# Fixing the order of the last rows on VectorE, with output gates read from PSUM and an early small exponential, in a one-core hybrid decoder layer

## The chip, the cores and the metric

The kernel runs on one core of a Trainium2 chip. The metric is the device time of one execution in microseconds (us), lower is better. In the profile the core's engines are PE (TensorE, matrix products), PEld (its weight loads), DVE (VectorE), ACT (ScalarE), POOL (GpSimd) and SP (SyncE, which issues most DMAs). Each engine runs its own instructions strictly in its own order and waits for others by semaphores.

## The reference

One layer of a decoder, for a prompt of 512 rows and for 8 samples of 4 rows each (32 sample rows), with a model width of 1024, all in float32. Cut to what matters:

```python
h = rms_norm(x, g_mix_pre); z = h @ w_in                   # mLSTM q, k, v, o, gates; attention q, k, v
h_ml = rms_norm(mlstm(q, k, v, gates), g_ml_head) * sigmoid(o)      # o: the output gates, 4 heads x 128
h_da = rms_norm(diff_attend(rope(dq), rope(dk), dv), g_da_head) * (1 - lam_init)
x = x + rms_norm(concat(h_ml, h_da) @ w_out, g_mix_post)
q = rms_norm(x, g_mem_pre) @ w_mq                           # 4 heads x 256
p = softmax(q @ mk.T / 16)                                  # 256 memory tokens; samples: a cached mk and mv each
x = x + rms_norm((p @ mv) @ w_mo, g_mem_post)
u = rms_norm(x, g_ffn_pre) @ w_up                           # 2 x 2752 columns
c = causal_depthwise_conv3(u); a, g = split(c)
x = x + rms_norm((silu(g) * a) @ w_down, g_ffn_post)        # the last line is the tail
# rms_norm(x, g) = x * (mean(x*x) + 1e-6) ** -0.5 * g
```

For the prompt, mk and mv are computed from 256 memory tokens that are normed first (the memory norm). The outputs are the new rows, and the keys, values and states of the layer.

## The kernel before

The 512 prompt rows are four row groups of 128 (b = 0 to 3), and the 32 sample rows are group 4. Weights are streamed from memory. A DMA on SP brings a 512 KB piece into a staging tile `wst`; ACT casts it to a reduced type (line L146), and DVE takes the rest (`split`, L147) into a weight tile `wslot`. Every product is computed as three matmuls, high times high and the two mixed ones. The class `Weights` (`W`) holds four such slots and issues the next load when one is freed; `W.last` is the last weight DMA issued.

Instructions of each engine are put in order by a scheduler from the order of the code, buffers and its own estimates. `tc.issue_after(x)` says that what stands inside may not be put ahead of instruction x; `tc.high_priority()` and `burst` move pieces forward. Generators (`yield`) interleave stages. Tiles come from pools that turn around a few buffers: `N` (5 wide row tiles), `T2`, `Z`, `sm` (small columns), `S` (11 large ones), and PSUM tiles `mm` and `at`.

The places in question are these.

- *Root of the mean square.* `rstd` returns a small tile `rs` with the sum raised to the power -0.5 on POOL (L304). The memory norm at the start copies it on DVE into `mrs` (L540, twice); the norm behind cross-attention copies it into `rsd` (L1178, five times).
- *Output gates.* The projection gives `soT`, four heads x 544 columns, from PSUM by an ACT copy per head and part (`ev_T`, L659). Later `out_gate` takes the sigmoid of each head on ACT (L1031), followed by a product on POOL. The prompt's differential attention then runs: keys are transposed on PE into `tpk` and copied out as `kT` (L1230, ACT and DVE in turn), and exponentials are taken by ACT (`da_soft`, L1261). Sigmoid and exponential need different function tables on ACT, so an ACT_TABLE_LOAD stands between them.
- *Cross-attention.* `ch_soft(i)`, i = 0 to 7 (head and pair of row groups): scores on PE (`sca`), the maximum on DVE (`cnm`), exponentials on ACT, the reciprocal (`csu`) and the shares `cp` on DVE (L1465); `ch_turn` then transposes `cp` on PE (`cpt`, L1474), and `ch_out` multiplies by the values (`cpo`). In between lies the same attention of the samples. The cached keys of sample b arrive as two tiles of 128 x 1024 (`wst` for b < 3, `kvt` from 3 on), are turned in 32 x 32 blocks on DVE (`mk_turn`, L1508), and PE takes the scores `ssc` from them (L1528). `ql` is the low part of the queries (L1439).
- *The tail.* The last group of weight pieces of `w_down` closes the row sums `yp` (prompt) and `ys` (samples). `chunk(b, n0)` is 12 matmuls for one row group and half of the columns, 512 wide; the last half, of group 3, is done as two pieces of 256. `add_y` adds the PSUM tile to `yp` or `ys` on DVE (L1884), ACT takes the square with its row sum `yss` (L1896), and `zy`, the product with the gain g_ffn_post, is taken by POOL for the first half and by DVE for the second (L1898). The sample rows lie on four partition ranges; ACT copies two of each half into `yf` (L1888), DVE copies the others into `yft` (L1890) and adds them (L1891). `end(b)` adds the two sums with epsilon on DVE (L1958, for the last group L1946 and L1947), takes the root on POOL, and adds `zy * rs` to the rows `xf`: by ACT and POOL (L1964, L1965) for the first halves of groups 0 and 1, otherwise by one DVE instruction (L1967, L1955). Each half is written out by a DMA on SP. The rows come back before that (`x_back`, L1975): two groups early, three more after the last weights, in the order 4, 0, 1, 2, 3.

PE's order in the tail is (0, 0), (4, 0), (4, 512), (0, 512), then both halves of groups 1, 2 and 3. The code states DVE's work per row group; the scheduler sets its order.

Of the kernel before, what the change touches and what calls it, by code (L numbers as in the profile page):

```python
# [77 lines left out]
def kernel(ctx: ExitStack, tc: tile.TileContext, I, O):  # L78
# [219 lines left out]
    def rstd(ss, n, w, dim, name="rs"):  # L298

        r = small(w, name)  # L300
# [3 lines left out]
        GTT(out=r[:n], in0=ss, in1=mhalf[:n, :w], op=ALU.pow)  # L304
# [724 lines left out]
    def out_gate():  # L1029
        for h in range(H):  # L1030
            ACT(out=soT[:, h], in_=soT[:, h], func=AF.Sigmoid)  # L1031
# [87 lines left out]
    def proj_add(xt, gname, src, gname2, dst, order=None, scale=None):  # L1119
# [52 lines left out]
        def rows_of(x, n, c0):  # L1172
# [5 lines left out]
            VCP(out=rs[:n], in_=rstd(sumsq(x, n, Z("sqx").bitcast(BF16)[:n]), n, 1, DM))  # L1178
# [266 lines left out]
    pTs, cps, scored = {}, {}, [None]  # L1445

    def ch_soft(i):
# [16 lines left out]
        for j in range(2):  # L1464
            VTS(out=p[:, j, :], in0=p[:, j, :], scalar1=su[:, j:j + 1], scalar2=None, op0=MUL)  # L1465
# [387 lines left out]
    for gi, js in enumerate(groups):  # L1853
# [21 lines left out]
        def add_y(b, ps, n0, w=512):  # L1875
# [9 lines left out]
            if b == 4 and last:  # L1885
                for e in range(2):
                    c = slice(n0 + 256 * e, n0 + 256 * e + 256)
                    nc.scalar.copy(out=yf[:, c], in_=y[NS * e:NS * e + NS])  # L1888
                    t = T2([NS, 256], "yft")
                    VCP(out=t, in_=y[64 + NS * e:64 + NS * e + NS])  # L1890
                    VTT(out=yf[:, c], in0=yf[:, c], in1=t, op=ADD)  # L1891
            if last:
                n = rows(b)[1]
                y = y if b < 4 else yf[:, n0:n0 + 512]
                ss = yss[b, n0] = sm.tile([P, 1], F32, name="yss", tag="yss", bufs=7)[:n]
                ACT(out=Z("sqj")[:n, :w], in_=y, func=AF.Square, scale=DM ** -0.5, accum_out=ss)  # L1896
                z = zs[b, n0] = T2([P, w], "zy")[:n]
                (VTT if n0 else GTT)(out=z, in0=y, in1=gf[:n, n0:n0 + w], op=MUL)  # L1898

        yss, zs = {}, {}  # L1900
        if last:
            yf = N("yf")[:NS]
# [25 lines left out]
        wd = []  # L1928

        def chunk(b, n0):  # L1930
            while len(wd) < (nk // 2 if n0 == 0 else nk):
# [1 line left out]
            w = 256 if (b, n0) == (TORD[-1], 512) else 512
            for o in range(0, 512, w):
                ps = mmp()[:, :w]
                for i in range(0, nk, 2 if b == 4 else 1):
                    t = one(b, ps, i, wd[(n0 and nk // 2) + i // 2], slice(o, o + w))
                add_y(b, ps, n0 + o, w)
            return t

        def end(b):
            c0, n = rows(b)
            xb = xf[b]
            out = O["y_prompt"][0, c0:c0 + n, :] if b < 4 else O["y_sample"].rearrange("b t d -> (b t) d")
            if b == TORD[-1]:
                VTT(out=yss[b, 0], in0=yss[b, 0], in1=yss[b, 512], op=ADD)  # L1946
                STT(out=yss[b, 768], in0=yss[b, 0], scalar=EPS, in1=yss[b, 768], op0=ADD, op1=ADD)  # L1947
# [115 lines left out]
```

## Time and profile before

| | |
|---|---|
| median of 3 runs | 935.84 us (933.85 to 938.36) |
| the profiled execution | 933.45 us |
| its span in the trace | 931.7 us |
| granted TensorE clock, mean | 0.996 |
| PE busy | 913.5 us, 98% |
| DVE busy | 606.5 us, 65% |
| ACT busy | 377.7 us, 41% |
| POOL busy | 223.0 us, 24% |
| moved by DMA | 130.59 MB, mean 140 GB/s |

The span is the time from the first to the last instruction that the trace shows; the profiled execution's own time is 1.75 us longer, and 2.39 us below the median of the runs. Busy times are sums over an engine's instructions. In a row of the timeline stand the start in the span, the busy time of the row, the engine, the line, the operation, what it writes and reads, its shape and how many instructions the row joins, and in brackets how long the engine was idle before it and what released it.

### The profile page before, as it was taken

The numbers are of one execution on the slowest core, as the hardware profiler recorded it, in microseconds if no ns is written. First come the engines' busy times: TensorE is split into PE (matmuls) and PEld (weight loads), VectorE is DVE, ScalarE is ACT, GpSimd is POOL, SyncE is SP. The second block draws the span as 40 slices with busy tenths as digits, with TensorE's granted clock in tenths as the row PEclk, the third lists the DMA queues.
The fourth block names the chain that finished last, engine by engine and source line by source line (L and its number), as shares of the span: only waits on it lengthen the run. The fifth ranks groups of instructions, "written<-read, shape, count | busy, mean of one in ns | idle before, by whom it ended". The sixth has DMA issues, their size and how long they took to land. (4 is left out here: it accounts for less than half of the span.)

```text
span 931.7 us, 17473 instructions
## 1 busy us (share of the span) xinstructions
PE 913.5 (98%) x6780; PEld 797.6 (86%) x6780; DVE 606.5 (65%) x1128; ACT 377.7 (41%) x728; POOL 223.0 (24%) x475
## 2 busy tenths in 40 slices
PE   9999999999999999999999999999999999999995
PEld 6899787879866778998877899899888998999974
DVE  5845144565888338768645878547748775776767
ACT  5745233344587437724534533322212221222232
POOL 6611000034442126581000642001001110110114
PEclk9999999999999999999999999999999999999998
DMA  9960023335780439966777631152044304412023
GB/s 284 313 192 4 1 91 139 91 102 164 237 294 19 136 107 293 300 214 236 293 244 194 200 108 53 38 168 69 27 137 137 91 4 131 122 47 91 25 94 118
DMA packets 120834, 130.59 MB, mean 140 GB/s; under 512 B 8599, under 2 KB 86264, under 8 KB 120752
## 3 DMA queue, kind: packets, MB, share of 16 engines
q1 hardware_dynamic: 114568, 125.96, 42.9%
q10 hardware_dynamic: 6184, 3.53, 1.2%
q8 instruction: 53, 0.87, 0.4%
q14 instruction: 29, 0.24, 0.1%
HBM read 112.54 MB, written 16.93 MB: 139 GB/s over the span
## 5 line engine op out<-in xcount | busy, mean ns | idle before, releaser
L485 PE MATMUL mm<-fT,wslot 128*128 128x256 f32 x1872 | 235.9, 288 | 0.0
L485 PEld LDWEIGHTS mm<-fT,wslot 128*128 128x128 f32 x1872 | 234.4, 188 | 1.8 <-issue 0.8
L146 ACT CAST wslot<-wst 128x1024 fp32r<-128x1024 f32 x125 | 130.4, 1049 | 255.0 <-issue 72.5
L147 DVE TENSOR_TENSOR wslot<-wst,wslot 128x1024 fp32r<-128x1024 f32 x125 | 154.2, 1239 | 76.1 <-ACT wslot L146 75.7
L1869 PE MATMUL mm<-wslot,act 128*128 128x512 f32 (+1 forms) x180 | 69.3, 387 | 0.0
L1872 PE MATMUL mm<-wslot,act 128*128 128x512 f32 (+1 forms) x172 | 67.1, 391 | 0.0
L1873 PE MATMUL mm<-wslot,act 128*128 128x512 f32 (+1 forms) x172 | 66.8, 392 | 0.0
L1771 POOL COPY cvo<-u 128x2 f32<-128x2 f32 x43 | 10.4, 242 | 217.4 <-DVE u L1769 217.4
L411 PE MATMUL mm<-wslot,hT 128*128 128x512 f32 x128 | 51.3, 402 | 0.0
L413 PE MATMUL mm<-wslot,hT 128*128 128x512 f32 x128 | 51.0, 399 | 0.0
L485 PE MATMUL mm<-hT,wslot 128*128 128x256 f32 (+1 forms) x384 | 50.9, 289 | 0.0
L412 PE MATMUL mm<-wslot,hT 128*128 128x512 f32 x128 | 50.8, 397 | 0.0
L1766 DVE TENSOR_TENSOR u<-mm,rsb 128x256 f32<-128x256 f32 x43 | 18.1, 424 | 48.4 <-PE mm L485 48.4
L485 PEld LDWEIGHTS mm<-hT,wslot 128*128 128x128 f32 x384 | 49.2, 188 | 0.5 <-issue 0.2
L1869 PEld LDWEIGHTS mm<-wslot,act 128*128 128x128 f32 x180 | 34.3, 191 | 8.0 <-issue 0.4
L1873 PEld LDWEIGHTS mm<-wslot,act 128*128 128x128 f32 x172 | 32.3, 188 | 6.9 <-issue 0.4
L1872 PEld LDWEIGHTS mm<-wslot,act 128*128 128x128 f32 x172 | 32.3, 188 | 6.9
L1783 ACT ACTIVATE c<-c 128x560 f32<-128x560 f32 x21 | 14.1, 672 | 57.2 <-DVE c L1777 57.1
L1777 DVE SCALAR_TENSOR_TENSOR c<-u,cvT,c 128x560 f32<-128x560 f32 x43 | 34.4, 799 | 0.9
L1776 DVE SCALAR_TENSOR_TENSOR c<-u,cvT,c 128x560 f32<-128x560 f32 x43 | 34.1, 794 | 0.2
L1884 DVE TENSOR_TENSOR yp<-mm,yp 128x512 f32<-128x512 f32 (+1 forms) x41 | 27.1, 673 | 4.5 <-PE mm L1873 4.3
L413 PEld LDWEIGHTS mm<-wslot,hT 128*128 128x128 f32 x128 | 24.1, 188 | 5.0
(497 smaller groups left out, 1857.5 us busy)
## 6 DMA issues: line engine op xcount, KB each, us to landing
wst<-in_w_up_dram SPq DMA_DIRECT2D x42, 512.0 KB
wst<-in_w_in_dram SPq DMA_DIRECT2D x28, 512.0 KB
wst<-in_w_down_dram SPq DMA_DIRECT2D x20, 512.0 KB
kvt<-in_cache_mem_k_dram SPq DMA_DIRECT2D x10, 512.0 KB
kvt<-in_cache_mem_v_dram SPq DMA_DIRECT2D x10, 512.0 KB
wst<-in_w_mk_dram SPq DMA_DIRECT2D x8, 512.0 KB
xb<-in_x_prompt_dram SPq DMA_DIRECT2D x8, 512.0 KB
wst<-in_cache_dk_dram SPq DMA_DIRECT2D x16, 256.0 KB
```

Source lines behind the costliest of these rows:

```text
L146: nc.scalar.copy(out=hi, in_=src)
L147: (eng or nc.vector).tensor_tensor(out=lo, in0=src, in1=f32(hi), op=SUB)
L411: mm(ps[b], lhsT=xt.hi(k, c0, c0 + n), rhs=s[:, 0, kk, :], start=(k == 0), stop=False)
L412: mm(ps[b], lhsT=xt.hi(k, c0, c0 + n), rhs=s[:, 1, kk, :], start=False, stop=False)
L413: return mm(ps[b], lhsT=xt.lo(k, c0, c0 + n), rhs=s[:, 0, kk, :], start=False, stop=(k == nk - 1))
L485: mm(ps[i], lhsT=s[:, l, k, :], rhs=x(k, c0, c1), start=(k == 0 and j == 0), stop=(k == 7 and j == 2))
L1776: STT(out=c, in0=u[:, 1:EXT - 1], scalar=w[1], in1=c, op0=MUL, op1=ADD)
L1777: STT(out=c, in0=u[:, 0:EXT - 2], scalar=w[0], in1=c, op0=MUL, op1=ADD)
L1869: mm(ps, lhsT=t[:, 0, c0:c0 + P], rhs=s[:, 0, i % 2, cs], start=st, stop=False)
L1872: mm(ps, lhsT=t[:, 0, c0:c0 + P], rhs=s[:, 1, i % 2, cs], start=False, stop=False)
L1873: return mm(ps, lhsT=t[:, 1, c0:c0 + P], rhs=s[:, 0, i % 2, cs], start=False, stop=en)
L1884: VTT(out=y, in0=ps, in1=y, op=ADD)
```

## The change

There are five parts.

1. `rstd` gets an argument `out`, and POOL writes the root where the copies (two to `mrs`, five to `rsd`) had put it. The copies are gone.
2. For heads 1 to 3 the output gate's sigmoid is taken by ACT straight from PSUM, in place of the copy and the later sigmoid. Head 0 is as before. Behind the last of these sigmoids ACT gets an exponential of one column (`tab`), whose result nobody reads.
3. The stream transposes of the cached keys of samples 3 to 7 are placed behind the shares of `ch_soft` 1, 2 and 3 (`shares[i]` is the second multiplication of round i).
4. All five reloads of the rows are issued together behind the last weight DMA, in the order 0, 1, 4, 2, 3; `yf` comes from pool `S` instead of `N`.
5. In the tail, each large DVE instruction is issued behind the one that the code names before it (`then`, which keeps the last one in `after`). All products with the gain go to DVE. The sample rows are copied by ACT in eight pieces, and DVE joins them by one addition of 512 columns per half. Sums with epsilon move from DVE to POOL. POOL and ACT keep the update of two pieces, (2, 0) and (3, 512). The last write-back is issued on ACT's queue.

The diff, cut to its core:

```diff
-    def rstd(ss, n, w, dim, name="rs"):
+    def rstd(ss, n, w, dim, name="rs", out=None):
...
-        GTT(out=r[:n], in0=ss, in1=mhalf[:n, :w], op=ALU.pow)
-        return r[:n]
+        out = r[:n] if out is None else out
+        GTT(out=out, in0=ss, in1=mhalf[:n, :w], op=ALU.pow)
+        return out
...
-        VCP(out=mrs[:, b:b + 1], in_=rstd(sumsq(xms[b], P, N("hN")), P, 1, DM))
+        rstd(sumsq(xms[b], P, N("hN")), P, 1, DM, out=mrs[:, b:b + 1])
...
+        def ev(i, c0, c1, ps):
+            t = ACT(out=soT[:, h, c0:c1], in_=ps, func=AF.Sigmoid)
+            if (h, i) == (H - 1, 1):
+                with tc.issue_after(t.ins):
+                    ACT(out=small(1, "tab"), in_=mhalf[:, 0:1], func=AF.Exp)
...
-            VCP(out=rs[:n], in_=rstd(sumsq(x, n, Z("sqx").bitcast(BF16)[:n]), n, 1, DM))
+            rstd(sumsq(x, n, Z("sqx").bitcast(BF16)[:n]), n, 1, DM, out=rs[:n])
...
-            VTS(out=p[:, j, :], in0=p[:, j, :], scalar1=su[:, j:j + 1], scalar2=None, op0=MUL)
+            shares[i] = VTS(out=p[:, j, :], in0=p[:, j, :], scalar1=su[:, j:j + 1], scalar2=None, op0=MUL)
...
-            if b:
-                mk_turn(b + 2)
-            mk_turn(b + 3)
+            with tc.issue_after(shares[b // 2 + 1].ins):
+                if b:
+                    mk_turn(b + 2)
+                mk_turn(b + 3)
...
+        def then(f, **kw):
+            with tc.issue_after(after[0].ins) if after[0] else nullcontext():
+                after[0] = f(**kw)
...
+        def root(b, n0s):
+            ss = yss[b, n0s[0]]
+            for o in n0s[1:]:
+                nc.gpsimd.tensor_scalar(out=yss[b, o], in0=yss[b, o], scalar1=ss, scalar2=EPS if o == 512 else 0.0,
+                                        op0=ADD, op1=ADD)
+                ss = yss[b, o]
+            roots[b] = rstd(ss, rows(b)[1], 1, None)
...
+        with tc.issue_after(W.last.ins):
+            for b in (0, 1, 4, 2, 3):
+                x_back(b)
...
+        times_g(*add_rows(1, 512, chunk(1, 512)[1]))
+        root(1, (0, 512))
+        for a in js4:
+            times_g(*a)
+        root(4, (0, 512))
+        times_g(*add_rows(2, 0, chunk(2, 0)[1]))
+        out_rows(1)
...
+        times_g(*add_rows(3, 512, chunk(3, 512, 256)[1], 256))
+        times_g(*add_rows(3, 768, chunk(3, 768, 256)[1], 256))
+        root(3, (0, 512, 768))
+        out_piece(2, 512)
+        out_piece(3, 512, 256, pool=True)
+        out_piece(3, 0)
+        out_piece(3, 768, 256, queue=nc.scalar.dma_start)
```

How the order of instructions changes is shown at three places. First ACT, where the output gates end and the differential attention begins. Before:

```order
L659 COPY soT<-mm 128x256
L659 COPY soT<-mm 128x288
L1031 ACTIVATE soT<-soT 128x544
L1230 COPY kT<-tpk 128x4x128
L1261 ACT_TABLE_LOAD
L1261 ACTIVATE pda,su<-sda,nm 128x128 x2
```

And now (L828 is the sigmoid from PSUM, L831 the small exponential, L1244 and L1275 are the former L1230 and L1261):

```order
L828 ACTIVATE soT<-mm 128x256
L828 ACTIVATE soT<-mm 128x288
L831 ACT_TABLE_LOAD
L831 ACTIVATE tab<-mhalf 128x1
L1244 COPY kT<-tpk 128x4x128
L1275 ACTIVATE pda,su<-sda,nm 128x128 x2
```

The table load has moved ahead of the first copy of `kT`, and the pass over 544 columns is gone.

Second DVE in cross-attention, from the first turn of a `kvt` tile on. Before:

```order
L1508 STREAM_TRANSPOSE kvt<-kvt 128x1024 x2
L1439 SCALAR_TENSOR_TENSOR ql<-mm,qh 128x256 x2
L1508 STREAM_TRANSPOSE kvt<-kvt 128x1024 x2
L1459 TENSOR_REDUCE cnm<-sca 128x2
L1463 RECIPROCAL csu<-csu 128x2
L1465 TENSOR_SCALAR cp<-cp,csu 128x256 x2
L1439 SCALAR_TENSOR_TENSOR ql<-mm,qh 128x256 x2
L1508 STREAM_TRANSPOSE wst<-wst 128x1024
L1508 STREAM_TRANSPOSE kvt<-kvt 128x1024 x2
L1459 TENSOR_REDUCE cnm<-sca 128x2
L1508 STREAM_TRANSPOSE kvt<-kvt 128x1024
L1463 RECIPROCAL csu<-csu 128x2
```

And now (L1453, L1473, L1477, L1479 and L1522 are the former L1439, L1459, L1463, L1465 and L1508):

```order
L1453 SCALAR_TENSOR_TENSOR ql<-mm,qh 128x256 x4
L1473 TENSOR_REDUCE cnm<-sca 128x2
L1477 RECIPROCAL csu<-csu 128x2
L1479 TENSOR_SCALAR cp<-cp,csu 128x256 x2
L1453 SCALAR_TENSOR_TENSOR ql<-mm,qh 128x256 x2
L1522 STREAM_TRANSPOSE wst<-wst 128x1024
L1473 TENSOR_REDUCE cnm<-sca 128x2
L1477 RECIPROCAL csu<-csu 128x2
L1479 TENSOR_SCALAR cp<-cp,csu 128x256 x2
L1522 STREAM_TRANSPOSE kvt<-kvt 128x1024 x2
L1453 SCALAR_TENSOR_TENSOR ql<-mm,qh 128x256 x2
L1473 TENSOR_REDUCE cnm<-sca 128x2
```

Four turns of `kvt` tiles stood ahead of the first maximum and four more around the second; now the first two stand behind the shares of the second round.

Third DVE at the very end, its last large instructions. Before:

```order
L1898 TENSOR_TENSOR zy<-yp,gb 128x512
L1958 SCALAR_TENSOR_TENSOR yss<-yss 128x1
L1967 SCALAR_TENSOR_TENSOR xf<-zy,rs,xf 128x512 x2
L1884 TENSOR_TENSOR yp<-mm,yp 128x512
L1884 TENSOR_TENSOR yp<-mm,yp 128x256
L1898 TENSOR_TENSOR zy<-yp,gb 128x256
L1884 TENSOR_TENSOR yp<-mm,yp 128x256
L1946 TENSOR_TENSOR yss<-yss 128x1
L1898 TENSOR_TENSOR zy<-yp,gb 128x256
L1947 SCALAR_TENSOR_TENSOR yss<-yss 128x1
L1955 SCALAR_TENSOR_TENSOR xf<-zy,rs,xf 128x512
L1955 SCALAR_TENSOR_TENSOR xf<-zy,rs,xf 128x256
```

And now (everything large is recorded at L1940, inside `then`):

```order
L1940 SCALAR_TENSOR_TENSOR xf<-zy,rs,xf 32x512 x2
L1940 TENSOR_TENSOR yp<-mm,yp 128x512
L1940 TENSOR_TENSOR zy<-yp,gb 128x512
L1940 TENSOR_TENSOR yp<-mm,yp 128x256
L1940 TENSOR_TENSOR zy<-yp,gb 128x256
L1940 TENSOR_TENSOR yp<-mm,yp 128x256
L1940 TENSOR_TENSOR zy<-yp,gb 128x256
L1940 SCALAR_TENSOR_TENSOR xf<-zy,rs,xf 128x512 x2
L1940 SCALAR_TENSOR_TENSOR xf<-zy,rs,xf 128x256
```

The updates of row group 2 (two of 128x512 in L1967) stood ahead of the last three adds. Now one of them is POOL's, and the other stands behind the last add and product, with no sum of DVE's in between.

More of the change, by code (lines that the diff above doesn't have):

```diff
@@ L1443 @@
     oT = XT("oT")
-    pTs, cps, scored = {}, {}, [None]
+    pTs, cps, scored, shares = {}, {}, [None], {}
     def ch_soft(i):
@@ L1884, in add_y @@
                 VTT(out=y, in0=ps, in1=y, op=ADD)
[L1885 to L1902, printed above, removed]
         if not last:
@@ L1927, with chunk @@
             continue
-        wd = []
-        def chunk(b, n0):
+        wd, yss, zs, roots, xf, after = [], {}, {}, {}, {}, [None]
+        yf = S([P, 2, 1024], F32, "yf")[:NS]
+        def chunk(b, n0, w=512):
             while len(wd) < (nk // 2 if n0 == 0 else nk):
                 wd.append(W.get())
[L1933 to L1939, printed above, removed]
@@ L1970, with square @@
-        xf = {}
+            ps = mmp()[:, :w]
+            half = n0 // 512
+            for i in range(0, nk, 2 if b == 4 else 1):
+                t = one(b, ps, i, wd[(half and nk // 2) + i // 2], slice(n0 - 512 * half, n0 - 512 * half + w))
+            return t, ps
+        def then(f, **kw):
+            with tc.issue_after(after[0].ins) if after[0] else nullcontext():
+                after[0] = f(**kw)
+        def square(b, n0, y, n):
+            ss = yss[b, n0] = sm.tile([P, 1], F32, name="yss", tag="yss", bufs=11)[:n]
+            ACT(out=Z("sqj")[:n, :y.shape[-1]], in_=y, func=AF.Square, scale=DM ** -0.5, accum_out=ss)
@@ new lines, in times_g, with add_rows, add_sample @@
+        def times_g(b, n0, y, n, w):
+            z = zs[b, n0] = T2([P, w], "zy")[:n]
+            then(VTT, out=z, in0=y, in1=gf[:n, n0:n0 + w], op=MUL)
+        def add_rows(b, n0, ps, w=512):
+            y = yp[b // 2][:, b % 2, n0:n0 + w]
+            then(VTT, out=y, in0=ps, in1=y, op=ADD)
+            square(b, n0, y, P)
+            return b, n0, y, P, w
+        def add_sample(n0, ps):
+            y = ys[:, n0 // 512]
+            then(VTT, out=y, in0=ps[:, :256], in1=y, op=ADD)
+            for e in range(2):
+                c = slice(n0 + 256 * e, n0 + 256 * e + 256)
+                for l in range(2):
+                    g = 64 * l + NS * e
+                    nc.scalar.copy(out=yf[:, l, c], in_=y[g:g + NS])
@@ new lines, in join_sample @@
+        def join_sample(n0):
+            y = yf[:, 0, n0:n0 + 512]
+            then(VTT, out=y, in0=y, in1=yf[:, 1, n0:n0 + 512], op=ADD)
+            square(4, n0, y, NS)
+            return 4, n0, y, NS, 512
+        def root(b, n0s):
[5 more added lines that the diff above has]
+            roots[b] = rstd(ss, rows(b)[1], 1, None)
@@ L1975, in x_back, with out_piece @@
             dma(out=xf[b], in_=xd[1][c0:c0 + n, :])
-        x_back(TORD[0])
-        x_back(TORD[1])
-        t = chunk(TORD[1], 0)
+        def out_piece(b, n0, w=512, pool=False, queue=dma):
+            c0, n = rows(b)
+            c, z, rs, xb = slice(n0, n0 + w), zs[b, n0], roots[b], xf[b]
+            out = O["y_prompt"][0, c0:c0 + n, :] if b < 4 else O["y_sample"].rearrange("b t d -> (b t) d")
+            if pool:
+                nc.scalar.mul(out=z, in_=z, mul=rs)
+                GTT(out=xb[:, c], in0=xb[:, c], in1=z, op=ADD)
+            else:
+                then(STT, out=xb[:, c], in0=z, scalar=rs, in1=xb[:, c], op0=MUL, op1=ADD)
+            queue(out=out[:, c], in_=xb[:, c])
```

67 lines of the change are left out of this document (26 added, 41 removed).

## The prediction

> **What bounds the kernel now.** I read the head of the page first, then the chain that ended last, then the end of the span stretch by stretch, and last the three places in the middle that the change touches.
>
> ```profile
> span 931.7 us, 17473 instructions
> PE 913.5 (98%) x6780; PEld 797.6 (86%) x6780; DVE 606.5 (65%) x1128; ACT 377.7 (41%) x728; POOL 223.0 (24%) x475
> ...
> PE 38%; DVE 3%; issue 1%; ACT 1%; POOL 0%; DVEq 0%; ACTq 0%; POOLq 0%
> ```
>
> PE is busy 913.5 of 931.7 us, and the change takes no matmul away that the reference needs. So the change can pay in PE's idle time alone, 18.2 us, and by no more than the part of it that it touches. The largest piece stands at the end (columns: stretch, its length, busy time and count on PE, PEld, DVE, ACT and POOL, granted clock, DMA share, GB/s):
>
> ```profile
> 900.00:905.00 5.00, 5.00 (x28) 3.54 (x27) 4.84 (x11) 3.26 (x8) 2.48 (x2) 1.00 0.25 101
> 915.00:920.00 5.00, 5.00 (x35) 4.58 (x33) 3.67 (x4) 2.10 (x5) 4.76 (x4) 1.00 0.37 144
> 920.00:925.00 5.00, 0.23 (x2) 0.02 (x1) 4.30 (x8) 1.19 (x5) 1.82 (x2) 0.99 0.46 171
> 925.00:931.70 6.70, 0.00 (x0) 0.00 (x0) 2.36 (x6) 1.02 (x3) 1.30 (x2) 0.50 0.22 78
> ```
>
> PE has finished by 920.23, and 11.5 us follow without it; from 920 to 925 it is DVE that works (4.30 of 5). The instructions there, in order of time on each engine (start, busy time, engine, line):
>
> ```profile
> 917.21 0.28 PE L1869 MATMUL mm<-wslot,act 128*128 128x256 f32 x1
> ...
> 919.95 0.28 PE L1873 MATMUL mm<-wslot,act 128*128 128x256 f32 x1
> ```
>
> ```profile
> 913.56 0.69 DVE L1898 TENSOR_TENSOR zy<-yp,gb 128x512 f32<-128x512 f32 x1
> 914.17 0.75 DVE L1967 SCALAR_TENSOR_TENSOR xf<-zy,rs,xf 128x512 f32<-128x512 f32 x1
> 914.83 0.15 DVE L1958 SCALAR_TENSOR_TENSOR yss<-yss 128x1 f32<-128x1 f32 x1
> ...
> 916.88 1.77 DVE L1967 SCALAR_TENSOR_TENSOR xf<-zy,rs,xf 128x512 f32<-128x512 f32 x1 [1.29 <-POOL rs L304]
> 918.57 0.68 DVE L1884 TENSOR_TENSOR yp<-mm,yp 128x512 f32<-128x512 f32 x1
> ...
> 924.72 0.41 DVE L1884 TENSOR_TENSOR yp<-mm,yp 128x256 f32<-128x256 f32 x1
> ...
> 926.66 1.61 DVE L1955 SCALAR_TENSOR_TENSOR xf<-zy,rs,xf 128x512 f32<-128x512 f32 x2 [0.73 <-POOL rs L304]
> ```
>
> ```profile
> 902.56 1.70 ACT L1888 COPY yf<-ys 32x256 f32<-32x256 f32 x4 [0.74 <-DVE ys L1884]
> ...
> 916.80 1.30 POOL L1898 TENSOR_TENSOR zy<-yp,gb 128x512 f32<-128x512 f32 x1
> ...
> 926.07 0.55 POOL L304 TENSOR_TENSOR rs<-yss,mhalf 128x1 f32<-128x1 f32 x1 [1.56 <-DVE yss L1947]
> ...
> 895.05 13.17 SPq L1975 DMA_DIRECT2D xf<-x_d  x3
> ...
> 927.43 1.69 SPq L1956 DMA_DIRECT2D out_dram<-xf  x3
> ```
>
> PE's last product is there at 920.23, but DVE adds it only at 924.72: 4.5 us of backlog. DVE stood idle 1.29 us before 916.88, waiting for POOL's root of an earlier row group, with an add ready in PSUM behind it; the update that then ran took 1.77 us, beside a POOL product of 1.30 us.
>
> **The tail: 4.75 us less.** The fixed order leaves PE's order alone, so 920.23 stays. Can DVE be up to date by then? The sample rows' two adds end about 902.86. From there the new order puts 21 operations ahead of the add of piece (3,0), whose last matmul comes just before 917.21: 15 adds, joins and products and 6 residual updates. From 913.56 to 914.17 is 0.61 a product, from 914.17 to 914.83 is 0.66 an update: 9.15 + 3.96 = 13.1. Two joins wait for eight ACT copies (1.70 per four, so until 905.96), some 0.6 more. The sum is 916.6, 0.6 of slack. After that PE sets the pace, and the last add can start at about 920.3, 4.4 earlier. The chain behind it keeps its length: square, sum, root at 926.07, updates at 926.66. The sum moves from DVE (0.15) to POOL, which no row shows; between 0.15 and POOL's 0.55 for the root, less the hop between engines, I take nothing. Another 0.35 comes from the last write-backs: three stood in a row on SP (1.69, 0.56 each), now the very last one goes out on ACT's queue; of the 0.56 I count most. 4.4 + 0.35 = 4.75. Bounds: 5.0 with all of the 0.56, and 2.6 if DVE's operations stay as long as their means (worked out among the rivals).
>
> Costed at nothing: the four DVE copies of sample rows become ACT copies, and ACT was busy 3.26 of 5 us there. All five reloads of x stand behind the last weight load on SP, where three stood (895.05); two that ran long before are added. Five are 2.18 MB; at the 101 GB/s of 900 to 905 the row groups are in at 900.2, 905.4, 906.7, 911.9 and 917.1, and by the prices above the order asks for the first at about 907.8 and for the last at about 922. No reload waits for a buffer any more, since yf has its own. If the loads were 5 us slower, the last updates would wait for them, and the gain would shrink one for one.
>
> **The output gates: 0.45 less.**
>
> ```profile
> 244.00 0.66 ACT L1031 ACTIVATE soT<-soT 128x544 f32<-128x544 f32 x1
> 245.21 0.59 ACT L1230 COPY kT<-tpk 128x512 f32<-128x512 f32 x1 [0.55 <-PE tpk L1229]
> 245.81 1.28 ACT L1261 ACT_TABLE_LOAD   x1
> 247.11 0.37 ACT L1261 ACTIVATE pda<-sda,nm 128x128 f32<-128x128 f32 x1
> ...
> 248.44 0.66 PE L1229 MATMUL tpk<-cpk,wst 128*128 128x128 f32 x4 [0.53 <-ACT kT L1230]
> ```
>
> Three gates lose an ACT pass of 0.66, and the last one stood before the kT copy. The table load of 1.28 stood between that copy and the first exponential. With the small exponential the load moves ahead of the copy, where ACT waited 0.55 for PE anyway: sigmoid done at 244.0, load until 245.3, copy until 245.9, first exponential near 246.05 rather than 247.11. PE waited 0.53 for ACT shortly after; that much at most goes at once, and a little more if later waits shrink too. I take 0.45, between 0 (the next wait, on DVE, takes its place) and 1.06, the exponential's whole shift.
> By the row the load costs 1.30 from its start to the next instruction. The Trainium skill, "ScalarE: Activation LUTs", section "What ACT_TABLE_LOAD costs", gives 1283 ns for the load and about 1380 ns of drain with it, 2.66 us a switch. The load agrees; the trace shows no drain between 245.81 and 247.11. By the page, hiding the whole switch would be an estimated 1.4 us more for this term, 929.1 in all, much as in the third rival below.
>
> **Roots written in place: 0.4 less.**
>
> ```profile
> 539.01 0.16 DVE L1178 COPY rsd<-rs 128x1 f32<-128x1 f32 x1 [0.95 <-POOL rs L304]
> ...
> 540.47 12.81 PE L472 MATMUL mm<-fT,wslot 128*128 128x288 f32 x96 [0.29 <-ACT fT L146]
> ```
>
> ```profile
> 13.96 0.50 PE L412 MATMUL mm<-wslot,memT 128*128 128x512 f32 x1 [0.39 <-DVE wslot L223]
> ```
>
> Five copies of roots go in the post-norm, two in the memory norm. One held DVE 0.95 us ahead of work that PE waited 0.29 for at 540.47: 0.3 to 0.35. Of the other post-norm copies none has a PE wait behind it. The memory norm's pair (0.15 each) stands ahead of the work that ends the 0.39 wait at 13.96: 0.05. Bounds 0 and 0.7, the sum of the two waits.
>
> **Cached K transposed later: 0.3 more.**
>
> ```profile
> 421.27 2.51 DVE L1508 STREAM_TRANSPOSE kvt<-kvt 128x1024 f32<-128x1024 f32 x2 [2.02 <-DMA kvt<-in_cache_mem_k_dram]
> ...
> 432.07 1.22 DVE L1508 STREAM_TRANSPOSE kvt<-kvt 128x1024 f32<-128x1024 f32 x1
> 433.21 0.63 DVE L1465 TENSOR_SCALAR cp<-cp,csu 128x256 f32<-128x256 f32 x2
> ...
> 433.71 0.74 PE L1474 MATMUL cpt<-cpk,cp 128*128 128x128 f32 x4 [0.67 <-DVE cp L1465]
> ```
>
> ```profile
> 430.00:440.00 10.00, 9.28 (x263) 8.06 (x261) 9.87 (x20) 7.46 (x30) 2.78 (x9) 1.00 0.58 197
> 440.00:450.00 10.00, 10.00 (x170) 8.91 (x171) 5.98 (x16) 6.04 (x21) 0.11 (x1) 1.00 1.01 407
> ```
>
> ```profile
> L1508 DVE STREAM_TRANSPOSE kvt<-kvt 128x1024 f32<-128x1024 f32 x10 | 12.2, 1228 | 4.3 <-DMA kvt<-in_cache_mem_k_dram 4.3
> ```
>
> Ten transposes now stand behind the softmax shares of their round. It gains PE's wait of 0.67 at 433.71: the transpose at 432.07 no longer stands ahead of the shares at 433.21. It costs cover: four transposes (4.9 us, two of them at 421.27) used to run while DVE waited for data, and now fall into 430 to 448. There DVE had 0.13 us free until 440 and 4.02 after. So they fit, but only just: laid out by hand at 1.17 a transpose, the last tile is ready at about 447.7, where PE, by its work ahead of them in the new order, would come to these four tiles near 446 and need about 2 us for them. Since it can start on the first tile before the last is ready, it runs behind by some 1.0 in all, less the 0.67: plus 0.3. Bounds: minus 0.7 (the wait goes, nothing comes in its place) and plus 4.2 (the 4.9 bare, less 0.67). I take a value near the lower end, since the 4.02 free after 440 lies nearest to where the transposes land.
>
> **The sum.** -4.75 - 0.45 - 0.4 + 0.3 = -5.3. The profiled execution took 933.45 with its span of 931.7, so it becomes 928.15 (span 926.4). The median of the runs shown is 935.84, 2.39 above the profiled execution; carried along, the forecast is 930.5. Half a per cent, about what a measurement can tell from no change, is 4.68 us, so the border is 931.16 and the forecast lies just past it.
>
> **The rivals.**
> Transposes become PE's wait: the middle of those bounds for the step, 2.3 lost rather than 0.3, half-way between 0.3 and 4.2. For it speaks that DVE is 99% busy from 430 to 440, so that every wait for a root or an exponential there is not made good; against it the 4.02 free after 440. 930.5 + 2.0 = 932.5, from 931.6 to 934.4 (the whole 4.2).
>
> The DVE operations of the tail stay long.
>
> ```profile
> L1967 DVE SCALAR_TENSOR_TENSOR xf<-zy,rs,xf 128x512 f32<-128x512 f32 (+1 forms) x6 | 5.3, 914 | 2.6 <-POOL rs L304 2.6
> L1898 DVE TENSOR_TENSOR zy<-yp,gb 128x512 f32<-128x512 f32 (+1 forms) x5 | 4.2, 837 | 0.1
> ```
>
> At these means, 0.16 above a short product (0.68) and 0.18 above a short update (0.73), ten products and six updates before the last add cost 1.6 + 1.1, less the 0.6 of slack: 2.1 of the 4.4 lost, 932.6. Against it: the long ones lie beside POOL's products, which leave. The Trainium skill, "SBUF — State Buffer", section "Who interferes with whom", calls DVE's and GpSimd's shared port pair an exclusive lock, which a DVE operation with two SBUF inputs takes; the update of 1.77 beside POOL's 1.30 agrees. That rule also speaks against the change in one place, since the sums and the root now run on POOL beside an update of row group 2 on DVE: an estimate by it is up to 0.7 more at the end.
>
> The middle gives more: gates at 1.06, transposes at -0.7, which is 1.6 less: 928.9. For it speaks that the transposes' loads come long before they are used; against it that DVE is full.
>
> Slower: PE waits for the transposes one after another. All ten exposed are 12.2 us; the 0.67 counts no more as a gain, the other terms give 5.6, so 935.84 + 12.2 - 5.6 = 942.4 at worst. It is no gain any more from five transposes on (6.1) and slower by half a per cent from 10.3 us, which is nine; with a DVE chain that slips as a whole, or with loads of the caches pushed back by buffers that come free later, it could come there. Against it: PE has a good deal of other work in this order.
>
> **How the numbers follow.** My forecast 0.56, transposes 0.20, long operations 0.10, more from the middle 0.08, slower or level by the transposes 0.06. Of the first, its own range 928.7 to 932.3, about a fifth (0.11) lies above 931.16. Faster: 0.45 + 0.08 = 0.53. Within: 0.11 + 0.20 + 0.10 + 0.02 = 0.43. Slower: 0.04. For 8 in 10 the range goes from 927.8, below the middle's 928.9 by the write-backs' and the last chain's unknowns, to 934.0, past both rivals near 932.5.
>
> **What would show it.** The last add starts within 0.5 us of PE's last matmul, and the last updates near 922.3 on the old time scale. DVE's products take 0.6 to 0.7 throughout and no update waits over 0.5 for x. The table load stands before the first kT copy and PE's 0.53 wait is gone. The 0.95 before the root's copy is gone, PE's 0.29 with it. Between 430 and 450 PE is idle 0.5 to 1.5 in sum, with the scores of the cached K as what waits. The prediction is wrong if PE loses over 2 us there, or if the last add still comes 2 us after PE's end.

## The result and the profile after

The changed kernel took 930.49 us (median of 5 runs, 929.37 to 930.87) against 934.81 for the kernel before (5 runs). The ratio is 0.995, with a 95% interval of 0.9933 to 0.9967. The forecast was 930.5 with a range of 927.8 to 934.0. So the time came out as forecast, but the terms behind it did not: the tail gave about half of its term (2.64 of 4.75), the output gates gave twice theirs (1.03 against 0.45).

The head of the page after, and the same stretches as before:

```profile
span 928.8 us, 17454 instructions
PE 912.6 (98%) x6780; PEld 796.8 (86%) x6780; DVE 602.0 (65%) x1115; ACT 377.4 (41%) x729; POOL 219.9 (24%) x475
...
900.00:905.00 5.00, 5.00 (x28) 3.52 (x27) 3.65 (x6) 3.63 (x9) 0.00 (x0) 1.00 1.00 320
915.00:920.00 5.00, 5.00 (x34) 4.43 (x32) 4.93 (x9) 1.39 (x5) 1.91 (x3) 1.00 0.35 123
920.00:925.00 5.00, 0.02 (x1) 0.00 (x0) 4.10 (x8) 2.30 (x8) 2.99 (x5) 0.84 0.31 113
925.00:928.80 3.80, 0.00 (x0) 0.00 (x0) 0.72 (x1) 0.00 (x0) 0.44 (x1) 0.50 0.39 138
```

The span fell by 2.9 us, from 931.7 to 928.8; the profiled execution took 930.63. DVE now stands idle for part of 900 to 905 (busy 3.65 of 5, before 4.84) and is full from 915 to 920 (4.93, before 3.67), and from 920 on it still works 4.10 of 5 us without PE. The rows of the tail, on DVE:

```profile
902.97 0.68 DVE L1940 TENSOR_TENSOR zy<-yp,gb 128x512 f32<-128x512 f32 x1
905.86 0.69 DVE L1940 TENSOR_TENSOR yp<-mm,yp 128x512 f32<-128x512 f32 x1 [2.21 <-PE mm L1888]
...
918.95 0.67 DVE L1940 TENSOR_TENSOR yp<-mm,yp 128x512 f32<-128x512 f32 x1
...
920.26 0.42 DVE L1940 TENSOR_TENSOR yp<-mm,yp 128x256 f32<-128x256 f32 x1
920.72 1.10 DVE L1940 TENSOR_TENSOR zy<-yp,gb 128x256 f32<-128x256 f32 x1
921.74 0.41 DVE L1940 TENSOR_TENSOR yp<-mm,yp 128x256 f32<-128x256 f32 x1
922.19 0.42 DVE L1940 TENSOR_TENSOR zy<-yp,gb 128x256 f32<-128x256 f32 x1
922.53 0.75 DVE L1940 SCALAR_TENSOR_TENSOR xf<-zy,rs,xf 128x512 f32<-128x512 f32 x1
924.11 1.61 DVE L1940 SCALAR_TENSOR_TENSOR xf<-zy,rs,xf 128x512 f32<-128x512 f32 x2 [0.83 <-POOL rs L305]
```

On POOL, and the last write-back on ACT's queue:

```profile
920.28 1.26 POOL L1990 TENSOR_TENSOR xf<-xf,zy 128x512 f32<-128x512 f32 x1 [0.83 <-ACT zy L1989]
...
922.92 0.51 POOL L1974 TENSOR_SCALAR yss<-yss 128x1 f32<-128x1 f32 x1 [0.94 <-ACT sqj L1944]
923.52 0.56 POOL L305 TENSOR_TENSOR rs<-yss,mhalf 128x1 f32<-128x1 f32 x1
...
925.76 0.34 ACTq L1993 DMA_DIRECT2D out_dram<-xf  x1
```

PE ends at 920.02, and the last add starts at 921.74, 1.7 us later; it was to start at once. Three things are to be read here. DVE idled 2.21 us in front of the add at 905.86, waiting for PE. The product at 920.72 took 1.10 us where its equal at 922.19 took 0.42, and POOL's update of 1.26 us runs beside it. And from the last add to the last updates it is 2.37 us (921.74 to 924.11), where it was 1.94 before (924.72 to 926.66), because the sum on POOL takes 0.51 beside DVE's update of 922.53.

At the output gates:

```profile
244.67 1.28 ACT L831 ACT_TABLE_LOAD   x1
245.97 0.20 ACT L831 ACTIVATE tab<-mhalf 128x1 f32<-128x1 f32 x1
246.08 0.57 ACT L1244 COPY kT<-tpk 128x512 f32<-128x512 f32 x1
246.73 0.37 ACT L1275 ACTIVATE pda<-sda,nm 128x128 f32<-128x128 f32 x1
```

The load stands ahead of the copy, and PE's wait of 0.53 behind it is gone.

To see where time goes, every matmul of one trace was paired with the same one of the kernel before, in order, and their starts subtracted. PE's lead or delay against the kernel before, step by step, in us (minus is earlier; the last column is the span less PE's end):

| kernel | at 30 us (start) | gained at the gates, 240 to 250 | in cross-attention, 400 to 470 | at the roots, 530 to 545 | after PE's end |
|---|---|---|---|---|---|
| before | 0 | 0 | 0 | 0 | 11.44 |
| changed | +0.68 | -1.03 | +0.26 | -0.61 | 8.81 |
| e1_mrs_back | -0.30 | -1.03 | +0.31 | -0.61 | 8.80 |
| e2_turn_early | +1.13 | -1.04 | +0.49 | -0.55 | 8.80 |
| e3_tail_only | +0.05 | 0.00 | -0.35 | -0.04 | 8.80 |
| e4_pe_order | +1.36 | -1.03 | +0.54 | -0.61 | 7.14 |
| e5_no_exp | +0.45 | -0.01 | -0.08 | -0.62 | 8.82 |
| e6_rsd_back | +0.79 | -1.04 | -0.50 | -0.03 | 8.81 |
| e7_all_dve | +0.59 | -1.03 | -0.60 | -0.61 | 7.15 |
| e8_best | +0.61 | -1.04 | +0.46 | -0.62 | 7.15 |
| e9_mk_dve | -0.56 | -1.03 | -0.23 | -0.61 | 7.15 |
| e10_mrs_dve | +1.04 | -1.03 | +0.47 | -0.61 | 7.15 |

Each row is one profiled execution. The columns of the gates, the roots and the tail repeat to 0.07 us. The start and cross-attention do not: they spread over 1.9 and 1.1 us, also between kernels that are the same there. The start is not over at 30 us: e1_mrs_back, e5_no_exp, e9_mk_dve and e10_mrs_dve lose another 0.3 to 0.4 us by 60.

### The profile page after: what moved, and what is told of

The parts are those of the page before. It is cut to its first block, busy times and chain, and to the rows that moved or that the text cites. A ratio compares the mean times of both kernels' runs of the same rounds, so it can differ in the third digit from the quotient of the medians.

```text
span 928.8 us, 17454 instructions
## 1 busy us (share of the span) xinstructions
PE 912.6 (98%) x6780; PEld 796.8 (86%) x6780; DVE 602.0 (65%) x1115; ACT 377.4 (41%) x729; POOL 219.9 (24%) x475
## 4 chain that ended last, share of the span: by engine, by line
PE 94%; DVE 3%; DMA 1%; issue 1%; ACT 0%; POOL 0%; DVEq 0%; POOLq 0%; ACTq 0%
PE mm L486 33%; PE mm L413 8%; PE mm L414 8%; PE mm L412 8%; PE mm L473 8%; PE mm L1884 4%; PE mm L1888 4%; PE mm L1887 4%; PE mm L391 2%; PE sda L1271 2%; PE tp L333 1%; PE sca L1469 1%; PE cpo L1500 1%; PE oda L1299 1%; PE sdn L391 1%; PE ssc L1542 1%
## 5 line engine op out<-in xcount | busy, mean ns | idle before, releaser
L414 PEld LDWEIGHTS mm<-wslot,hT 128*128 128x128 f32 x128 | 24.1, 188 | 5.0
L413 PEld LDWEIGHTS mm<-wslot,hT 128*128 128x128 f32 x128 | 24.1, 189 | 4.8
```

The source lines that it names most:

```text
L413: mm(ps[b], lhsT=xt.hi(k, c0, c0 + n), rhs=s[:, 1, kk, :], start=False, stop=False)
L414: return mm(ps[b], lhsT=xt.lo(k, c0, c0 + n), rhs=s[:, 0, kk, :], start=False, stop=(k == nk - 1))
```

## The experiments

e1 to e4 were timed side by side, so were e5 to e8, and e9 with e10, each time with the kernel before between them, in 5 to 7 runs each. Theory 1 and the rival are those of the expectation that stands ahead of each result.

**The tail alone (e3_tail_only).** The changed kernel with parts 1, 2 and 3 undone:

```diff
-        rstd(sumsq(xms[b], P, N("hN")), P, 1, DM, out=mrs[:, b:b + 1])
+        VCP(out=mrs[:, b:b + 1], in_=rstd(sumsq(xms[b], P, N("hN")), P, 1, DM))
...
-          gemmB(hT, [ev_out(h) for h in range(H)]))
+          gemmB(hT, [ev_T(soT, h) for h in range(H)]))
...
-            rstd(sumsq(x, n, Z("sqx").bitcast(BF16)[:n]), n, 1, DM, out=rs[:n])
+            VCP(out=rs[:n], in_=rstd(sumsq(x, n, Z("sqx").bitcast(BF16)[:n]), n, 1, DM))
...
-            with tc.issue_after(shares[b // 2 + 1].ins):
-                if b:
-                    mk_turn(b + 2)
-                mk_turn(b + 3)
+            if b:
+                mk_turn(b + 2)
+            mk_turn(b + 3)
```

(`out_gate` takes all four sigmoids again.)

> The kernel before with the tail alone changed (fixed DVE order, sample copies on ACT, reloads together, sums on POOL, last write-back on ACT's queue); PE's order is that of before throughout. Theory 1: the tail pays 2.7 us, read from the two traces as 928.8 - 920.0 = 8.8 us after PE's last matmul against 11.5 before, so the span is about 929.0 with PE's end at 920.2, and the last add starts 1.7 us after PE's end. Rival, the prediction's: 4.75 us, a span near 927.0. Rival 2: part of the 2.7 is owed to the other parts; then less than 2 us.

Measured: 931.83 us against 934.43, ratio 0.9970 (0.9959 to 0.9982); the span is 928.7, and PE's end is at 919.93. What follows PE is 8.80 us instead of 11.44: the tail pays 2.64, as the first theory says. The forecast's 4.75 is out, and nothing of the 2.64 is owed to the other parts, since the figure is the same in all six kernels with this tail.

**PE's order (e4_pe_order).** One constraint more in the changed kernel:

```diff
-        times_g(*add_rows(0, 512, chunk(0, 512)[1]))
+        t, ps = chunk(0, 512)
+        times_g(*add_rows(0, 512, ps))
...
-        times_g(*add_rows(1, 0, chunk(1, 0)[1]))
+        with tc.issue_after(t.ins):
+            ps = chunk(1, 0)[1]
+        times_g(*add_rows(1, 0, ps))
```

> The changed kernel with one more constraint: PE's matmuls of chunk (1,0) stand behind the last of chunk (0,512). In the changed kernel the two are mixed and end together, near 905.8 and 906.0, and DVE idles 2.21 us in front of the first of their adds. Theory 1: DVE's backlog at the end comes from that idle time. Then (0,512) ends near 903.7, DVE uses most of the 2.2 us, the last add starts within 0.4 us of PE's end rather than 1.7 after it, and the span is 1.0 to 1.6 us shorter, about 927.5. Rival: the backlog comes from DVE operations that wait beside POOL's (the product of 1.10 us at 920.72); then the last add still comes over 1 us after PE's end, and at most 0.4 us is gained.

Measured: 928.97 us, ratio to the kernel before 0.9934 (0.9921 to 0.9948); span 928.1. On DVE:

```profile
904.22 0.69 DVE L1940 TENSOR_TENSOR yp<-mm,yp 128x512 f32<-128x512 f32 x1 [0.26 <-PE mm L1888]
...
919.98 0.98 DVE L1940 TENSOR_TENSOR zy<-yp,gb 128x256 f32<-128x256 f32 x1
920.95 0.42 DVE L1940 TENSOR_TENSOR yp<-mm,yp 128x256 f32<-128x256 f32 x1
```

The wait of 2.21 has shrunk to 0.26, and the last add starts 0.04 us after PE's end at 920.91, although the product of 0.98 beside POOL's update is still there. What follows PE is 7.14 us, 1.67 less. PE itself lost 0.16 between 890 and 910 in this execution; with the same order e7_all_dve and e8_best lost nothing there, e9_mk_dve 0.25 and e10_mrs_dve 0.17, so whether the order has a price of its own can't be told. The backlog came from PE's order, which leaves the two chunks to end together. The rival, that the long operations make the backlog, falls: they cost 0.6, and once DVE is up to date they are covered. The span itself fell by only 0.7, because this execution started 0.68 later and lost 0.28 more in cross-attention.

**POOL's two updates given to DVE (e7_all_dve).** On top of e4_pe_order:

```diff
-        out_piece(2, 0, pool=True)
         times_g(*add_rows(3, 512, chunk(3, 512, 256)[1], 256))
+        out_piece(2, 0)
...
-        out_piece(3, 512, 256, pool=True)
         out_piece(3, 0)
+        out_piece(3, 512, 256)
         out_piece(3, 768, 256, queue=nc.scalar.dma_start)
```

> The kernel with PE's chunk (0,512) first (e4_pe_order), and in the tail the two updates that ACT and POOL had, (2,0) and (3,512), are given to DVE, (2,0) behind the product of (3,512). Theory 1, the engines' shared port: POOL's update of 1.26 us cost DVE 0.55 to 0.7 at the product beside it (0.98 to 1.10 instead of 0.42), and POOL's of 0.75 cost 0.6 at the last two updates (1.62 instead of 1.0). Then DVE does one 512 update more (0.67) and one 256 (0.35) at no cost: the last three updates take 1.4 us together, the span is 0.1 to 0.3 us shorter than e4_pe_order's 928.1 when set to the same start. Rival: POOL's help was worth its work; then the span is 0.5 to 1 us longer.

Measured: 928.42 us, ratio 0.9931 (0.9916 to 0.9945).

```profile
917.87 0.43 DVE L1940 TENSOR_TENSOR zy<-yp,gb 128x256 f32<-128x256 f32 x1
918.21 0.75 DVE L1940 SCALAR_TENSOR_TENSOR xf<-zy,rs,xf 128x512 f32<-128x512 f32 x1
918.88 0.42 DVE L1940 TENSOR_TENSOR yp<-mm,yp 128x256 f32<-128x256 f32 x1
...
921.25 1.54 DVE L1940 SCALAR_TENSOR_TENSOR xf<-zy,rs,xf 128x512 f32<-128x512 f32 x3 [0.83 <-POOL rs L305]
```

The product is back at 0.43, the update of (2, 0) fits into the time that this frees, and three updates at the end take 1.54 where two beside POOL took 1.62. What follows PE is 7.15, the same as in e4_pe_order. So POOL's help was worth nothing (DVE does both pieces in the same time), but taking it away gained nothing either: the first theory's 0.1 to 0.3 did not show. The span of 926.0, 2.1 below e4_pe_order's, is not this edit's: the same program was 0.77 earlier at the start and 1.14 better in cross-attention.

**The small exponential (e5_no_exp).**

```diff
-            t = ACT(out=soT[:, h, c0:c1], in_=ps, func=AF.Sigmoid)
-            if (h, i) == (H - 1, 1):
-                with tc.issue_after(t.ins):
-                    ACT(out=small(1, "tab"), in_=mhalf[:, 0:1], func=AF.Exp)
+            ACT(out=soT[:, h, c0:c1], in_=ps, func=AF.Sigmoid)
```

> The changed kernel without the one-column exponential; the sigmoids still come from PSUM. The table load then stands between the first copy of kT and the first exponential again; no other instruction moves. From the output gates to the attention the changed kernel gained 0.95 to 1.15 us on PE (0.65 to 0.85 behind at 245.85, 0.30 ahead at 249.6). Theory 1: the earlier load carries most of that, so that without it PE is 0.6 to 1.0 us later from 250 us on. Rival: the missing ACT pass of 0.66 carries it; then the exponential is worth under 0.3 us.

Measured: 931.36 us against 930.55 for e6_rsd_back, timed beside it; span 929.6. On ACT:

```profile
246.07 0.58 ACT L1241 COPY kT<-tpk 128x512 f32<-128x512 f32 x1 [1.23 <-PE tpk L1240]
246.67 1.28 ACT L1272 ACT_TABLE_LOAD   x1
247.96 0.37 ACT L1272 ACTIVATE pda<-sda,nm 128x128 f32<-128x128 f32 x1
```

ACT stands idle for 1.23 ahead of the copy, and the load comes behind it again. PE gains 0.01 at the gates, against 1.03 in every kernel with the exponential. Without the early load the saved passes gain nothing: they only lengthen ACT's wait for PE's transposes, from 0.55 to 1.23. But that is the stretch into which the load of 1.28 then goes. With the pass of 0.66 still in place the load would have found 0.55 us of idle time; no run has the exponential without the saved passes, so how much of the 1.03 the load would gain alone is open.

**The roots behind cross-attention (e6_rsd_back).** The five copies put back, as in the diff of e3_tail_only.

> The changed kernel with the five copies of roots behind cross-attention put back (rsd<-rs). Theory 1, as forecast: PE's wait of 0.29 for fT returns near 540, and PE is 0.3 to 0.6 us later from there on, of which some 0.2 is made good by 556. Rival: as at the start, removing copies moved something else and the net is zero or a loss; then PE is not later, or earlier, without them.

Measured: 930.55 us; span 928.5. The two rows of PE, first of the changed kernel, then of this one:

```profile
540.04 2.23 PE L473 MATMUL mm<-fT,wslot 128*128 128x288 f32 x15
```

```profile
539.69 2.52 PE L473 MATMUL mm<-fT,wslot 128*128 128x288 f32 x17 [0.32 <-ACT fT L146]
```

The wait is back, and the step from 530 to 545 is -0.03 instead of -0.61. The copies' removal gains 0.58 there, more than the 0.29 that stood in the bracket: the bracket counts from the end of the matmul before, and without the wait PE would not have come to that end. The four matmuls ahead of it start 0.11 us apart and take 0.27 each. PE's lead jumps by 0.53 at the one matmul that stood at 540.47.

The 0.2 that PE loses again by 560 is lost in this kernel too, so it does not belong to the roots. It is lost in all kernels but e3_tail_only, which alone has the old output gates; in the changed kernel the matmuls from 547.5 to 552.5 start 0.133 us apart on average instead of 0.130. Why was not found. In the runs' medians the gain can't be seen (930.55 against 930.49 of another comparison).

**Transposes as before (e2_turn_early).** The constraint on `mk_turn` taken away, as in the diff of e3_tail_only.

> The changed kernel without the constraint on the transposes of the cached keys; the order on DVE, PE and ACT in cross-attention is then that of the kernel before. Theory 1: the constraint gained PE 0.7 us at the first transposed shares and gave 0.6 of it back by the end of cross-attention, so without it the span changes by 0.0 to 0.2 us and PE's wait of 0.67 for the shares is back. Rival: it cost or brought more than the single pair of traces shows, 1 us or more either way.

Measured: 930.84 us, ratio 0.9958 (0.9945 to 0.9972), beside 929.93 for e1_mrs_back; span 929.3. PE's old wait of 0.67 for the shares did not come back: the first transposes of `kvt` tiles began at 419.51 here, at 421.27 in the kernel before, and the shares at 432.00 instead of 433.21. In its place PE stood twice in front of the scores of the cached keys, for nothing that the profile names:

```profile
436.90 0.47 PE L1542 MATMUL ssc<-wst,qx 128*32 128x64 f32 x18 [0.70 <-issue]
...
443.62 1.29 PE L1542 MATMUL ssc<-kvt,qx 128*32 128x128 f32 x36 [0.46 <-issue]
```

The first of these waits is in the changed kernel too:

```profile
436.75 0.47 PE L1542 MATMUL ssc<-wst,qx 128*32 128x64 f32 x18 [0.76 <-issue]
```

From 400 to 470 the nine executions with the constraint lie between -0.60 and +0.54, mean +0.07; the three with the old order at 0, -0.35 and +0.49. No effect of the constraint can be told from this spread.

What these waits are can be read from the traces, though no run was made to vary it. PE's instructions are themselves brought by DMA, on a queue of their own (packets, MB, share of 16 engines):

```profile
q8 instruction: 53, 0.87, 0.4%
```

These are 53 packets of 16,384 bytes, some 63 bytes for each of PE's 13,740 instructions in the trace. Ten of the twelve traces, all but the kernel before and e3_tail_only, have such waits in front of `ssc`, 15 in all, from 0.16 to 1.38 us. Each stands in front of PE's 6338th or 6594th instruction, which are 256 apart, about what one packet holds, and each ends 1.35 to 1.60 us after a packet of this queue has landed. In the other two traces PE comes to the 6338th 1.37 and 1.63 us after the packet has landed, and no such wait shows. So PE waits here, as far as the traces tell, for its next instructions: what it gains shortly ahead of such a place it can lose again there. The sum of PE's waits between 400 and 470, less the 0.67 of the kernel before, comes within 0.3 us of the table's column in nine of the eleven changed kernels.

**The start (e1_mrs_back, e8_best, e9_mk_dve, e10_mrs_dve).** e1_mrs_back puts the two copies `mrs<-rs` back, as in the diff of e3_tail_only; e8_best does so on top of e7_all_dve.

> The changed kernel with the two DVE copies of the memory norm's roots put back (mrs<-rs); nothing else differs. In the trace of the changed kernel the first weight and memory splits on POOL took 1.79 us each where they took 1.27 and 1.73 before, and PE came to the matmul that stood at 15.46 before 0.51 us later. Theory 1, the copy of 0.14 us set who came first: without it DVE's half of the split starts before POOL's, and POOL waits behind it. Then with the copies PE is back at the old times from 16 us on (within 0.2 us), POOL's first split is near 1.27 again, and the span is 0.6 to 0.9 us shorter, about 928.1. Rival: the later start is the spread of the first loads from one execution to the next; then the copies change nothing, POOL's split stays 1.79, and the span stays 928.5 to 929.

Measured for e1_mrs_back: 929.93 us, ratio 0.9955 (0.9942 to 0.9969), span 927.9; PE is 0.98 earlier at 30 us than in the changed kernel, of which 0.69 is left at 60. The first halves of a weight piece's low part, in the changed kernel and in e3_tail_only, which has the copies:

```profile
7.76 0.69 DVE L223 TENSOR_TENSOR wslot<-wst,wslot 128x512 fp32r<-128x512 f32 x1
...
7.80 1.79 POOL L223 TENSOR_TENSOR wslot<-wst,wslot 128x512 fp32r<-128x512 f32 x1 [0.66 <-ACT wslot L221]
```

```profile
7.70 1.27 POOL L223 TENSOR_TENSOR wslot<-wst,wslot 128x512 fp32r<-128x512 f32 x1 [0.66 <-ACT wslot L221]
...
7.74 1.78 DVE L223 TENSOR_TENSOR wslot<-wst,wslot 128x512 fp32r<-128x512 f32 x1
```

Whoever starts first, by 0.04 us, runs at its own speed; the other lasts until both are done. With the copies POOL came first in three executions of four, without them in none of six (e9 and e10, which have no halves, left out). The fourth is e8_best.

> The kernel of e7_all_dve with the two copies of the memory norm's roots put back (e1_mrs_back). If the gains add up: 0.8 to 0.9 from the start, 1.5 from PE's order and 0.1 to 0.3 from the updates against the changed kernel's 928.8, a span near 926.2 and a median near 928. If they do not add, the start's 0.8 is lost again in a wait on the first weights, and the span is about 927.

Measured for e8_best: 928.86 us, ratio 0.9936 (0.9920 to 0.9951), span 927.0. Here the gain did not show: with the copies PE is 0.61 behind at 30 us, no better than e7_all_dve without them, and the medians (928.86 and 928.42) stand the other way round. In this execution the first weights came later (their cast began at 7.21 instead of 6.49 in e1_mrs_back), and DVE was first again. Of five executions with copies the cast began at 6.49, 6.54, 6.58, 6.77 and 7.21; of seven without, between 6.68 and 7.45. Part of the difference in the table is thus the arrival of the first loads.

Not all of it is. In the changed kernel PE has a wait that the kernel before does not have:

```profile
15.96 0.50 PE L414 MATMUL mm<-wslot,memT 128*128 128x512 f32 x1 [0.71 <-POOL memT L147]
```

It is there, with 0.71 or 0.72, in all six kernels that lack the copies and share the halves, in no other, and costs PE 0.88 to 0.90. The wait of 0.39 at 13.96, which the prediction looked at, is gone in the same six and gives back 0.55. At like times of the first cast the kernels with the copies are ahead at 30 us: the kernel before (6.77) by 0.45 and 0.59 of e5_no_exp (6.78) and e7_all_dve (6.80), e8_best (7.21) by 0.18 and 0.75 of e6_rsd_back and e4_pe_order (7.21 too). How the copies come to matter for POOL's `memT` was not followed further.

e9_mk_dve takes the race away:

```diff
-        slotsA(w_mk, n0, True)
+        slotsA(w_mk, n0)
```

> The kernel of e7_all_dve, and the low parts of the first eight weight pieces (the memory keys' weights) are taken by DVE alone in one instruction of 1024 columns instead of half each by DVE and POOL. In all ten traces so far the two halves start within 0.05 us of each other or overlap, and one of them lasts as long as both together: DVE 0.69 and POOL 1.79, or POOL 1.27 and DVE 1.6 to 1.78. Theory 1, the port is held by one at a time: the halves take 1.8 us together, DVE alone takes 1.24, and PE is 0.3 to 0.8 us earlier at 30 us than in executions without the root copies whose first weights come at the same time (0.45 to 1.36 behind the kernel before). Rival: sharing helped and DVE has too much else to do there; then PE is later by 0.5 us or more.

Measured: 928.77 us, ratio 0.9939 (0.9924 to 0.9953); span 925.9.

```profile
8.05 1.23 DVE L147 TENSOR_TENSOR wslot<-wst,wslot 128x1024 fp32r<-128x1024 f32 x1 [0.40 <-ACT wslot L146]
```

DVE alone takes 1.23 us for what the two took 1.8 us for, and PE is 0.56 ahead of the kernel before at 30 us (0.24 at 60), with first weights cast at 6.97, later than in the changed kernel (6.68). The port theory holds for the pieces; yet the median does not differ from e7_all_dve's.

> The kernel of e9_mk_dve with the two copies of the memory norm's roots put back on DVE. Theory 1: what the copies changed was who comes first at the port for the first halves; with DVE alone for the weights there is no such race, and the copies cost or bring less than 0.3 us at 30 us. Rival: the copies help in another way; then PE is 0.5 us or more earlier at 30 us than in e9_mk_dve, with the first weights at the same time.

Measured: 928.82 us, ratio 0.9935 (0.9921 to 0.9949), span 928.0. PE is 1.04 behind at 30 us, the other side from both expectations. The second weight piece came late: ACT waited 1.04 us for its DMA until 11.47, where e9_mk_dve began that cast at 10.76. The run tells nothing on the copies. Over many executions it is not settled whether removing the two copies costs anything: the traces speak for 0.2 to 0.75 us at 30 us where the two engines share the halves, the medians say -0.56 (e1_mrs_back against the changed kernel) and +0.44 (e8_best against e7_all_dve), both within the spread of the runs.

**A better version.** Five kernels with PE's order fixed took 928.42 to 928.97, 0.6 to 0.7% below the kernel before and 1.5 to 2.1 us below the changed kernel, which was timed separately; among these five no difference can be measured. All five still have the last sum on POOL.

## Why the prediction was right, point by point

*The time.* That 930.49 meets 930.5 so closely is luck. Terms that repeat from trace to trace are the tail (-2.64), the gates (-1.03), the roots (-0.58) and the loss by 560 (+0.20): -4.05. The medians fell by 4.32. The forecast had -5.3 from a median of 935.84, which became 934.81 with two runs more; the two differences cancelled. Between the two profiled executions the span fell by only 2.9, since the start (+0.68), cross-attention (+0.26) and the stretch from 470 to 530 (+0.26) went against the changed one; "2.39 carried along" compared a fast execution of the kernel before with its median.

*The tail, -4.75: the direction was right, and so was the mechanism (DVE's backlog behind PE's end), the size was not.* The step that failed is "From there the new order puts 21 operations ahead of the add of piece (3,0)", with "0.6 of slack": it counted DVE's work from 902.86 on without asking when PE would deliver. PE mixes chunks (0, 512) and (1, 0), which end together near 906, and the fixed order puts the add of (0, 512) second. The trace of the kernel before had it already, in a row that joins the last matmuls of both:

```profile
905.63 0.64 PE L1873 MATMUL mm<-wslot,act 128*128 128x512 f32 x2
```

DVE idled 2.21 us there, and the last add came 1.65 us later than forecast against PE's end. The second miss is "I take nothing" for the sum on POOL, where the rivals allowed up to 0.7: it cost 0.43 (2.37 against 1.94). 4.75 - 1.65 - 0.43 = 2.67. Of the write-backs' 0.35 some 0.30 came: from the end of the last update to the end it is 3.10 us (925.72 to 928.82) against 3.40 (928.27 to 931.67). The 2.64 also meets the forecast's lower bound of 2.6, but that one was worked out for long DVE operations; e4_pe_order gets 1.67 back with those still in place.

*The reloads and ACT's copies at nothing:* right. The window from 900 to 905 moved 320 GB/s instead of 101, and no update waits for `xf`.

*The gates, -0.45: too small.* The value was taken from PE's next wait of 0.53, and 1.06, the exponential's whole shift, was only the bound. The shift went through to PE almost whole (1.03): 0.69 at the wait of 0.53 itself, since a bracket understates a wait (e6_rsd_back), the rest within the next 1.5 us, where a wait for DVE shrank too. The saved ACT passes, named first in that part, were worth nothing without the early load (e5_no_exp).
By the row the load is followed by the next instruction after 1.30 us (244.67 to 245.97). The Trainium skill, "ScalarE: Activation LUTs", section "What ACT_TABLE_LOAD costs", has a drain of about 1380 ns beside the load; no trace here shows it, and the gain of 1.03 stays below the load alone.

*The roots, -0.4: right in kind for the post-norm.* Its copies gave 0.58, above the 0.3 to 0.35 taken; the bound of 0.7 held only because it added the two brackets. The memory norm's 0.05 did not come: its wait of 0.39 went, but the new wait of 0.71 for POOL took more.

*The transposes, +0.3:* not told apart from nothing, mean +0.07 over nine executions. PE's wait of 0.67 is gone in the changed kernel, and DVE's transposes became PE's wait in one execution only (0.34 in e7_all_dve). What took the gain is PE's wait for its own instructions, a term that the prediction did not have; it did expect PE to be idle in front of the scores of the cached keys, but for late transposes.

*The rivals.* "The DVE operations of the tail stay long" was right in its mechanism at three places: 1.10 at 920.72, the two updates of 1.61 and POOL's sum of 0.51; the rest run at 0.69 and 0.75. The pairs of 7.70 and 7.74, and 7.76 and 7.80, agree with the Trainium skill, "SBUF — State Buffer", section "Who interferes with whom": the port pair that DVE and GpSimd share is an exclusive lock, and the order of issue decides who blocks. "The middle gives more" came true for the gates (1.03 of 1.06), not for the transposes. The slower case did not come near.

## What to carry to other kernels

A fixed order on one engine has to be laid against the times at which the engine before it delivers: a chain that has time enough in sum still starts late if its first link waits for two results that are ready together. When an engine waits right behind a function switch, moving the table load into an idle stretch can be worth most of the load (1.03 of 1.28 here); sparing instructions ahead of that stretch was worth nothing by itself, but made it as long as the load. DVE and POOL did not halve two-operand work between them. A wait's bracket can understate what its removal gains, and a wait without a releaser is worth a look at the queue that brings the instructions. Before a gain of one or two us is believed, each stage's time should be compared over several traces, since two of the five stages here spread by 1.9 and 1.1 us.

## What was not expected of the hardware

DVE and POOL on halves of the same work take 1.79 us where DVE alone takes 1.23, and 0.04 us of difference in their start decides which of them is the late one. A sum of 128 x 1 on POOL takes 0.19 us with DVE idle:

```profile
11.43 0.19 POOL L302 TENSOR_SCALAR rs<-ssq 128x1 f32<-128x1 f32 x1
```

The same instruction took 1.05 at 352.93 in the changed kernel, beside a DVE `split` that it outlasted by 0.05 us, and the last sum of the tail took 0.51 and ended 0.15 after DVE's update beside it. PE stood up to 1.4 us in front of small score matmuls, at places 256 instructions apart, until 1.35 to 1.60 us after the next 16 KB of its instructions had landed.
